# Moving query and key transposes to a projection bank, and leaving the projections two

## The chip, the cores and the metric

The kernel runs on one core of one Trainium2 chip. The metric is the device time of one execution in microseconds, from several runs; one further execution is profiled and gives the trace. In the profile the engines are PE (TensorE matmul, with PEld for its weight loads), DVE (VectorE), ACT (ScalarE), POOL (GpSimd) and SP (SyncE, which here issues most DMAs).

## The reference

One decoder layer over 512 tokens of width 1024, all in float32:

```
x = x + 0.5 * swiglu_ffn(x)                       # FFN 1
h = rms_norm(x)
fq, fk, fv, ff, dq, dk, dv, iq, ik, iw, ga, gb = split_columns(h @ w_in)
fq, fk = rms_norm(fq), rms_norm(fk)               # 8 heads of 64
o_a = fox_attention(fq, fk, fv, log_sigmoid(ff + b_forget))
o_b = dsa_attention(rms_norm(dq), rms_norm(dk), dv, iq, ik, iw, rel_bias)   # top-128 keys
x = x + (sigmoid(ga) * (o_a @ w_branch_a) + sigmoid(gb) * (o_b @ w_branch_b)) @ w_out
x = x + 0.5 * swiglu_ffn(x)                       # FFN 2
```

Each attention is causal: scores, a bias, softmax, and the weighted sum of values. `fox` has eight heads with their own keys and values, `dsa` eight heads that share one key and value head.

## The kernel before, in words

Every float32 operand is split in a high and a low part, and each product is three matmuls (`mm3`, lines 132 to 135: high by high, high by low, low by high). Tokens lie in four blocks of 128 (`NT`).

PSUM has eight banks of 128 x 512 floats. The kernel gives two to the tag `pt` (transposes), two to `s` (scores), one to `pv` (the sum of values, `po`) and three to `acc` (all products, through `acc_tile`). With three buffers under one tag, a new tile takes whichever buffer is free.

Between the two FFNs stands the mixing stage. The order of PE's instructions there is written out by hand; on the other engines a scheduler, which simulates the program when it is built, puts the instructions in order. The input projections and the later products are a list `units`, each a generator that yields after a few matmuls and says how long they take:

- unit 0: the small columns; 1 to 4: the indexer's queries (`fm_proj`, one bank each)
- 5 to 12: `fk0`, `fq0`, `fv0`, `fk1`, `fq1`, `fv1`, `dq0`, `dq1` (`tm_proj` through `tm256`, two banks each; the number is the half of the heads)
- then four gates, eight branch products, four more gates and four gates of the other branch (`fm_proj`, one bank each)

A `tm_proj` unit computes 512 tokens by 256 columns. Its first bank takes tokens 0 to 255, its second 256 to 511; it runs over two chunks of weights, in each over the four token blocks and four slices. So in the second chunk the first bank is complete eight product steps before the second. Then `done(ps)` reads the banks: `normed` scales them on ACT (L721), takes norms, and multiplies on POOL (L724); `values` reads each half bank once on ACT (L734) and once on DVE (L735).

`prod.run(us)` issues unit steps for about so many us between pieces of attention, `prod.finish(n)` runs units until n are done. The last steps before attention end unit 7 (`fv0`); a step that ends a unit may go on to the first product of the next one.

The attention loop goes over 16 heads `g` (8 fox, 8 dsa) and in each over four steps `s`, one query block each. A step does `value_step` (flip the probabilities of an earlier block by transposing into a `pt` bank, L925; copy them with ACT and DVE, L929 and L930; multiply by the values into `po`, L935 and L936), then `softmax_block` (scores into an `s` bank, L651 and L652; minimum on DVE, L914; exponential on ACT, L916; scaling on POOL, L918), then `prod.run(FILL[g])`. DVE also runs the selection of the top keys in between (L862, L864).

For every pair of heads, `get_q(g + 1)` transposes two heads' queries (`ps_q`, L626) into a `pt` bank, and reads them with ACT (L645) and DVE (L646) into `st`; `get_k(g + 1)` does so for the fox keys (`ps_k`, into `kh` and `kl`) and copies each half to the other partitions by DMA (L979, SP's queue). Before the change they follow steps 0 and 1 of every odd head. Weights are fetched three chunks ahead (`weight`, `load_w`: cast `wh` on ACT, L123; `wl`, on ACT at L125 with a DMA that adds, or on DVE or POOL at L128).

Of the kernel before, what the change touches and what calls it, by code (L numbers as in the profile page):

```python
# [18 lines left out]
P = 128  # L19
# [32 lines left out]
def tile_hybrid_layer(ctx: ExitStack, tc: tile.TileContext, a: dict):  # L52
# [10 lines left out]

    def acc_tile(name):
        return psum.tile([P, T], F32, tag="acc", bufs=3, name=name)

# [515 lines left out]
    with ExitStack() as merge_ctx, ExitStack() as mix_ctx, ExitStack() as att_ctx:  # L582
# [39 lines left out]

        def transposed(cols, name):
            ps = psum.tile([P, T], F32, tag="pt", bufs=2, name=name)
            for t in range(NT):
                PE.transpose(ps[:, t * P:(t + 1) * P], cols(t), ident)  # L626
            return ps
# [39 lines left out]

        def tm_proj(ws, cols, done):

            def run():  # L670
                ps = [acc_tile("ps_t")[:, :2 * cols].rearrange("p (u c) -> p u c", u=2) for _ in range(2)]
                for c in range(2):
                    wh, wl = ws[c]()
                    for t in range(NT):
                        for kk in range(4):
                            k = 4 * c + kk
                            mm3(ps[t // 2][:, t % 2], xh[k][:, t * P:(t + 1) * P], xl[k][:, t * P:(t + 1) * P],
                                wh[:, kk], wl[:, kk], k == 0 and t % 2 == 0, k == KD - 1 and t % 2 == 1)
                            if (c, t, kk) != (1, 3, 3):
                                yield MM / 2  # L680
                done(ps)
                yield MM / 2
            return run
# [14 lines left out]

        def small_done(ps):
            nonlocal rt  # L700
            rt = next(norm)
            for t in range(NT):
                p = ps[t // 2][:, t % 2]
                S.mul(sd[1][:, t], p[:, None, DH:2 * DH].to_broadcast([P, 2, DH]), rt[:, t:t + 1])
                S.mul(sg[:, t], p[:, 128:S_W], rt[:, t:t + 1])
                S.mul(sd[0][:, t], p[:, None, 0:DH].to_broadcast([P, 2, DH]), rt[:, t:t + 1])

                V.tensor_scalar(wi[:, t], sg[:, t, 72:80], rt[:, t:t + 1], DH ** -0.5 * H ** -0.5,
                                op0=OP.mult, op1=OP.mult)
# [4 lines left out]
        def normed(key):  # L714
            def done(ps):
                out = []
                for b in range(2):
                    kn = mp.tile([P, T], F32, tag="tn", bufs=8, name="kn")
                    kv = kn.rearrange("p (u c) -> p u c", u=2)
                    for u in range(2):  # L720
                        S.mul(kv[:, u], ps[b][:, u], rt[:, 2 * b + u:2 * b + u + 1])  # L721
                    r = qk_scale(kn, H)
                    kh = kn.rearrange("p (h d) -> p h d", d=DH)
                    G.tensor_mul(kh, kh, r[:, :, None].to_broadcast([P, H, DH]))  # L724
                    out.append(kv)
                tn[key] = out
            return done

        def values(hf):
            def done(ps):  # L730
                for t in range(NT):
                    vt = mp.tile([P, 4, P], F32R, tag=f"r{2 * t + hf}", name="fv")
                    src = ps[t // 2][:, t % 2].rearrange("p (h d) -> p h d", d=DH)
                    S.mul(vt[:, :, 0:DH], src, rt[:, t:t + 1])  # L734
# [19 lines left out]

        def tm256(name, n, done):
            return tm_proj([weight(a[name][n][:, 4 * c:4 * c + 4], 4, 256, W_AT, True) for c in range(2)], 256, done)

# [4 lines left out]
        units += [tm256("w_fk", 0, normed("fk0")), tm256("w_fq", 0, normed("fq0")), tm256("w_fv", 0, values(0)),  # L762
                  tm256("w_fk", 1, normed("fk1")), tm256("w_fq", 1, normed("fq1")), tm256("w_fv", 1, values(1)),
                  tm256("w_dq", 0, normed("dq0")), tm256("w_dq", 1, normed("dq1"))]
        n_fox = len(units)
# [185 lines left out]

        def columns(tiles, c, name):
            return transposed(lambda t: tiles[t // 2][:, t % 2, c * P:(c + 1) * P], name)

        def get_q(g):
# [3 lines left out]
            gain = gq[:, 0:1] if g < H else gq[:, 1:2]  # L959
            ps = columns(tn[f"{nm}{c // 2}"], c % 2, "ps_q")  # L960
            out = [at.tile([P, T], F32R, tag=tag, bufs=2, name="st") for tag in ("qh", "ql")]
# [5 lines left out]
        def get_k(g):  # L967
# [3 lines left out]
            c = g // 2  # L971
            ps = columns(tn[f"fk{c // 2}"], c % 2, "ps_k")
            out = []
# [71 lines left out]
        for g in range(2 * H):  # L1045
# [4 lines left out]
            for s in range(NT):  # L1050
# [10 lines left out]
                if g + 1 < 2 * H:  # L1061
                    if s == 0:
                        nb = get_bias(g + 1)
                    if s == 0 and g % 2:
                        nq = get_q(g + 1)
                    if s == 1 and g % 2:
                        nk = get_k(g + 1)
        for g, j in ((14, 3), (15, 0), (15, 1), (15, 2), (15, 3), (16, 0)):
            value_step(g, j)
            prod.run(FILL_LAST)  # L1070
        prod.finish(len(units))
        att_ctx.close()

# [118 lines left out]
```

## Time and profile before

| | us |
|---|---|
| median of 3 runs | 1090.99 (1089.07 to 1091.05) |
| the profiled execution | 1090.95 |
| its span, first to last instruction | 1088.9 |
| PE busy in the span | 1070.5 (98%) |
| DVE busy | 795.0 (73%) |
| ACT busy | 575.4 (53%) |
| POOL busy | 209.4 (19%) |
| mean granted TensorE clock | 0.998 |

A row of the trace names the line, the engine, the operation and, as out<-in, the tiles by the program's names; in brackets stands the idle time of the engine just before it and what ended that. `ps_t` and `ps_f` are the projection banks of `tm_proj` and `fm_proj`. A wait reads: who waited, at which line, for which engine's instruction.

### The profile page before, as it was taken

The page shows a single profiled execution, that of the slowest core. Times are in us where ns is not written, and L with a number is a line of the kernel's source. Part 1 is how long each engine was busy: PE and PEld are TensorE (multiplying, and loading weights), DVE is VectorE, ACT ScalarE, POOL GpSimd, SP SyncE. Part 2 cuts the span into 40 slices and gives each one's busy share as a digit, 9 for nine tenths or more (in the row PEclk, how much of TensorE's full clock was granted, in tenths as well). Part 3 has the DMA queues.
Part 4 walks back from the last instruction along what each step waited for, and adds up shares of the span by engine and source line. Part 5 has one row for each costly group of instructions (what it writes and reads, how often), then busy time and mean ns, then how long its engine had stood idle before and what let it go on. Part 6 is the DMA issues. An engine that isn't in the chain of part 4 may idle for free.

```text
span 1088.9 us, 17859 instructions
## 1 busy us (share of the span) xinstructions
PE 1070.5 (98%) x6880; PEld 968.1 (89%) x6880; DVE 795.0 (73%) x1287; ACT 575.4 (53%) x908; POOL 209.4 (19%) x280
## 2 busy tenths in 40 slices
PE   9999999999999999999999999999999999999998
PEld 7889899989998899988778778889998899989997
DVE  6896478755967489879764765879986588865974
ACT  5554155522555675877655785455663155522650
POOL 0000000000001316677752740000110001000100
PEclk9999999999999999999999999999999999999999
DMA  7434335523442268765124211425574356633552
GB/s 239 118 98 134 108 88 147 139 95 97 125 108 90 99 134 195 173 143 133 49 59 135 87 60 48 135 89 153 138 166 137 90 135 160 165 97 98 145 126 78
DMA packets 43572, 131.01 MB, mean 120 GB/s; under 512 B 5336, under 2 KB 5720, under 8 KB 43488
## 3 DMA queue, kind: packets, MB, share of 16 engines
q1 hardware_dynamic: 35120, 107.58, 32.5%
q0 software_dynamic: 8208, 22.02, 11.7%
q8 instruction: 54, 0.88, 0.3%
q10 hardware_dynamic: 160, 0.28, 0.1%
q14 instruction: 30, 0.25, 0.1%
HBM read 117.79 MB, written 2.11 MB: 110 GB/s over the span
## 4 chain that ended last, share of the span: by engine, by line
PE 85%; DVE 6%; ACT 4%; issue 2%; DMA 2%; POOL 1%; SPq 0%; DVEq 0%; POOLq 0%; ACTq 0%
PE pd L133 7%; PE pd L135 7%; PE pd L134 7%; PE pB L133 5%; PE pB L134 5%; PE pB L135 5%; PE pC L133 3%; PE pA L133 3%; PE pA L134 3%; PE pC L134 3%; PE pC L135 3%; PE pA L135 3%; PE ps_f L133 3%; PE ps_f L134 3%; PE ps_f L135 3%
## 5 line engine op out<-in xcount | busy, mean ns | idle before, releaser
L133 PE MATMUL pd<-ah,wh 128*128 128x512 f32 (+1 forms) x294 | 113.2, 385 | 0.0
L134 PE MATMUL pd<-al,wh 128*128 128x512 f32 (+1 forms) x294 | 113.1, 385 | 0.0
L135 PE MATMUL pd<-ah,wl 128*128 128x512 f32 (+1 forms) x294 | 113.1, 385 | 0.0
L112 ACT CAST wh<-s 128x1024 fp32r<-128x1024 f32 x57 | 60.1, 1054 | 99.1 <-PE pB L134 51.3
L133 PE MATMUL pB<-tbh,wh 128*128 128x256 f32 x304 | 85.0, 280 | 0.6 <-DVE u L435 0.6
L134 PE MATMUL pB<-tbl,wh 128*128 128x256 f32 x304 | 84.8, 279 | 0.0
L135 PE MATMUL pB<-tbh,wl 128*128 128x256 f32 x304 | 84.7, 279 | 0.0
L133 PE MATMUL ps_t<-wh,xh 128*128 128x256 f32 (+1 forms) x288 | 81.7, 284 | 0.0
L134 PE MATMUL ps_t<-wl,xh 128*128 128x256 f32 (+1 forms) x288 | 81.0, 281 | 0.0
L135 PE MATMUL ps_t<-wh,xl 128*128 128x256 f32 (+1 forms) x288 | 81.0, 281 | 0.0
L271 POOL DMA_DIRECT2D al<-gu x26 | 22.2, 856 | 260.5 <-ACT al L270 248.9
L113 DVE TENSOR_TENSOR wl<-s,wh 128x1024 fp32r<-128x1024 f32 x57 | 69.4, 1218 | 1.7 <-ACT wh L112 1.5
L393 POOL DMA_DIRECT2D s<-in_w_pair_dram x11 | 9.6, 877 | 297.9 <-DVE wl L113 297.9
L135 PEld LDWEIGHTS pd<-ah,wl 128*128 128x128 f32 x294 | 55.2, 188 | 11.1
L134 PEld LDWEIGHTS pd<-al,wh 128*128 128x128 f32 x294 | 55.2, 188 | 10.8
L133 PEld LDWEIGHTS pd<-ah,wh 128*128 128x128 f32 x294 | 55.2, 188 | 10.8
L133 PEld LDWEIGHTS pB<-tbh,wh 128*128 128x128 f32 x304 | 57.1, 188 | 1.1 <-issue 0.9
L134 PEld LDWEIGHTS pB<-tbl,wh 128*128 128x128 f32 x304 | 57.2, 188 | 0.0
L135 PEld LDWEIGHTS pB<-tbh,wl 128*128 128x128 f32 x304 | 57.2, 188 | 0.0
L134 PEld LDWEIGHTS ps_t<-wl,xh 128*128 128x128 f32 x288 | 55.1, 191 | 0.5
L133 PEld LDWEIGHTS ps_t<-wh,xh 128*128 128x128 f32 x288 | 55.0, 191 | 0.5
L135 PEld LDWEIGHTS ps_t<-wh,xl 128*128 128x128 f32 x288 | 55.0, 191 | 0.0
(355 smaller groups left out, 3611.9 us busy)
## 6 DMA issues: line engine op xcount, KB each, us to landing
rc<-in_w_pair_dram SPq DMA_DIRECT2D x16, 512.0 KB, 3.6
rb<-in_w_pair_dram SPq DMA_DIRECT2D x16, 512.0 KB, 3.6
ra<-in_w_pair_dram SPq DMA_DIRECT2D x15, 512.0 KB, 3.6
rd<-in_w_pair_dram SPq DMA_DIRECT2D x15, 512.0 KB, 3.7
re<-in_w_pair_dram SPq DMA_DIRECT2D x14, 512.0 KB, 3.7
al<-gu POOLq DMA_DIRECT2D x26, 256.0 KB, 4.7
s<-in_w_pair_dram POOLq DMA_DIRECT2D x11, 512.0 KB, 5.6
ra<-in_w_down_dram SPq DMA_DIRECT2D x7, 512.0 KB, 3.6
```

Of the source, the lines that this page charges most:

```text
L112: S.copy(wh[:, :f], raw[:, :f])
L113: V.tensor_sub(wl[:, :f], raw[:, :f], wh[:, :f].bitcast(F32))
L133: PE.matmul(out, lh, rh, start=start, stop=False, **more)
L134: PE.matmul(out, lh, rl, start=False, stop=False, **more)
L135: PE.matmul(out, ll, rh, start=False, stop=stop, **more)
L271: G.dma_start(l, u, accum_op=OP.add)
L393: G.dma_start(t["s2"], load["b"][2], accum_op=OP.add)
```

## The change

`acc_tile` no longer draws from a tag with three buffers: there are three tags `acc0`, `acc1`, `acc2` of one buffer each, taken in a fixed cycle or by name. The units `fk1`, `fq1`, `fv1`, `dq0` and `dq1` name acc0 and acc1, and set the cycle to these two, so that the gates and branch products after them use two banks as well; the cycle returns to three behind the attention loop. `get_q` and `get_k` for heads after the first transpose into acc2. Keys come first, after step 0 of an odd head, queries after step 2. `done(ps, b)` is called for each bank where its last product is issued. `get_k` makes sure that `fk1` is done before it reads it.

```diff
-    def acc_tile(name):
-        return psum.tile([P, T], F32, tag="acc", bufs=3, name=name)
+    acc_tags = {"next": cycle(("acc0", "acc1", "acc2"))}
+
+    def acc_tile(name, tag=None):
+        return psum.tile([P, T], F32, tag=tag or next(acc_tags["next"]), name=name)
...
-        def transposed(cols, name):
-            ps = psum.tile([P, T], F32, tag="pt", bufs=2, name=name)
+        def transposed(cols, name, tag=None):
+            ps = acc_tile(name, tag) if tag else psum.tile([P, T], F32, tag="pt", bufs=2, name=name)
...
-        def tm_proj(ws, cols, done):
+        def tm_proj(ws, cols, done, tags=(None, None)):
 
             def run():
-                ps = [acc_tile("ps_t")[:, :2 * cols].rearrange("p (u c) -> p u c", u=2) for _ in range(2)]
+                if tags[0]:
+                    acc_tags["next"] = cycle(tags)
+                ps = [acc_tile("ps_t", tag)[:, :2 * cols].rearrange("p (u c) -> p u c", u=2) for tag in tags]
...
-                            if (c, t, kk) != (1, 3, 3):
-                                yield MM / 2
-                done(ps)
-                yield MM / 2
+                            if (c, t % 2, kk) == (1, 1, 3):
+                                done(ps, t // 2)
+                            yield MM / 2
...
         units += [tm256("w_fk", 0, normed("fk0")), tm256("w_fq", 0, normed("fq0")), tm256("w_fv", 0, values(0)),
-                  tm256("w_fk", 1, normed("fk1")), tm256("w_fq", 1, normed("fq1")), tm256("w_fv", 1, values(1)),
-                  tm256("w_dq", 0, normed("dq0")), tm256("w_dq", 1, normed("dq1"))]
+                  *(tm256(name, n, done, ("acc0", "acc1"))
+                    for name, n, done in (("w_fk", 1, normed("fk1")), ("w_fq", 1, normed("fq1")), ("w_fv", 1, values(1)),
+                                          ("w_dq", 0, normed("dq0")), ("w_dq", 1, normed("dq1"))))]
...
-        def columns(tiles, c, name):
-            return transposed(lambda t: tiles[t // 2][:, t % 2, c * P:(c + 1) * P], name)
+        def columns(tiles, c, name, g):
+            return transposed(lambda t: tiles[t // 2][:, t % 2, c * P:(c + 1) * P], name, "acc2" if g else None)
...
-            ps = columns(tn[f"fk{c // 2}"], c % 2, "ps_k")
+            if c == 2:
+                prod.finish(9)
+            ps = columns(tn[f"fk{c // 2}"], c % 2, "ps_k", g)
...
                     if s == 0 and g % 2:
+                        nk = get_k(g + 1)
+                    if s == 2 and g % 2:
                         nq = get_q(g + 1)
-                    if s == 1 and g % 2:
-                        nk = get_k(g + 1)
...
         prod.finish(len(units))
+        acc_tags["next"] = cycle(("acc0", "acc1", "acc2"))
         att_ctx.close()
```

`small_done`, `normed` and `values` are split by bank in the same way: `values(hf)` reads the two token blocks of bank `b`, `normed(key)` appends one tile for each bank, and `small_done` does its work at the second.

More of the change, by code (lines that the diff above doesn't have):

```diff
@@ L697, in weight, with small_done @@
             return take
-        def small_done(ps):
+        def small_done(ps, b):
             nonlocal rt
+            if not b:
+                return
             rt = next(norm)
@@ L714, in normed, with done @@
         def normed(key):
[L715 to L726, printed above, removed]
+            def done(ps, b):
+                kn = mp.tile([P, T], F32, tag="tn", bufs=8, name="kn")
+                kv = kn.rearrange("p (u c) -> p u c", u=2)
+                for u in range(2):
+                    S.mul(kv[:, u], ps[b][:, u], rt[:, 2 * b + u:2 * b + u + 1])
+                r = qk_scale(kn, H)
+                kh = kn.rearrange("p (h d) -> p h d", d=DH)
+                G.tensor_mul(kh, kh, r[:, :, None].to_broadcast([P, H, DH]))
+                tn.setdefault(key, []).append(kv)
             return done
         def values(hf):
-            def done(ps):
-                for t in range(NT):
+            def done(ps, b):
+                for t in (2 * b, 2 * b + 1):
                     vt = mp.tile([P, 4, P], F32R, tag=f"r{2 * t + hf}", name="fv")
-                    src = ps[t // 2][:, t % 2].rearrange("p (h d) -> p h d", d=DH)
+                    src = ps[b][:, t % 2].rearrange("p (h d) -> p h d", d=DH)
                     S.mul(vt[:, :, 0:DH], src, rt[:, t:t + 1])
@@ L753, in keep_gate_b, with tm256 @@
             gb.append(g)
-        def tm256(name, n, done):
-            return tm_proj([weight(a[name][n][:, 4 * c:4 * c + 4], 4, 256, W_AT, True) for c in range(2)], 256, done)
+        def tm256(name, n, done, tags=(None, None)):
+            return tm_proj([weight(a[name][n][:, 4 * c:4 * c + 4], 4, 256, W_AT, True) for c in range(2)], 256, done,
+                           tags)
         oA = ([mp.tile([P, T], F32R, tag=f"oh{c}", name="oAh") for c in range(4)],
@@ L959, in get_q @@
             gain = gq[:, 0:1] if g < H else gq[:, 1:2]
-            ps = columns(tn[f"{nm}{c // 2}"], c % 2, "ps_q")
+            ps = columns(tn[f"{nm}{c // 2}"], c % 2, "ps_q", g)
             out = [at.tile([P, T], F32R, tag=tag, bufs=2, name="st") for tag in ("qh", "ql")]
```

## The prediction

> **What bounds the kernel now.** I read the page's busy shares first, then the waits of TensorE, then the timelines around the longest of them.
>
> ```profile
> PE 1070.5 (98%) x6880; PEld 968.1 (89%) x6880; DVE 795.0 (73%) x1287; ACT 575.4 (53%) x908; POOL 209.4 (19%) x280
> ```
>
> TensorE (PE) is busy for 1070.5 us of the span. Everything that this change can win lies in the other 18 us, and every new wait of PE adds to the end, because PE runs its instructions in the order written. The waits say who ends that idle time (columns: waiter, its line, whom it waited for; total us, times, longest):
>
> ```profile
> core 0 of [0], span 1088.9 us
> PE pt L925 <- DVE st L646: 2.7, 3, 1.7
> PE ps_qk L651 <- DVE mn L914: 2.2, 2, 1.2
> PE pt L925 <- DVE pl L930: 1.8, 3, 0.9
> PE po L936 <- DVE pl L930: 1.3, 3, 0.9
> PE po L935 <- DVE o L948: 1.1, 3, 0.6
> ...
> PE ps_k L626 <- DVE pl L930: 0.8, 1, 0.8
> ```
>
> All of these lie in the attention loop. The first row is the one that the change is about: a probability flip (`pt`) needs one of the two `pt` banks, and a bank still holds a transposed query until DVE has read it (`st`, L646). The third and the last row are the same conflict from other sides: a flip or the key transpose (`ps_k`) waits until DVE has emptied the other flip's bank (`pl`). One place of each kind, the second with what follows it:
>
> ```profile
> 452.80 0.66 PE L626 MATMUL ps_k<-ident,kn 128*128 128x128 f32 x4 [0.81 <-DVE pl L930]
> 454.18 0.55 PE L925 MATMUL pt<-ident,p 128*128 128x128 f32 x3 [0.72 <-DVE st L646]
> ...
> 561.31 0.55 PE L925 MATMUL pt<-ident,p 128*128 128x128 f32 x3 [0.93 <-DVE pl L930]
> 562.51 0.50 PE L935 MATMUL po<-ph,dvv 128*128 128x512 f32 x1 [0.65 <-DVE o L948]
> ```
>
> **Part 1: later queries and keys leave the `pt` banks.** Seven query and three key transposes go to bank acc2. The three rows `pt <- st`, `pt <- pl` and `ps_k <- pl` lose their cause: 2.7 + 1.8 + 0.8 = 5.3 us. That is the upper end; not all of it stays won. Behind 454.18 PE needs `pl` of the flip before it, behind 561.31 it waits for DVE again (0.65 us at `o`), and the row `po <- pl` (1.3 us) is DVE arriving late at the place where PE will now be earlier. I give back 1.3 us, the size of that row: net -4.0. Lower end: half is given back, -2.7; upper end: -5.3. The waits for `mn` (2.2) I leave where they are, since they are DVE's own lateness.
>
> **Part 2: keys in step 0, queries in step 2.** The same transposes, ACT copies and DVE subtractions run, only at another step; ACT takes 0.68 us and DVE 0.75 us for each half (rows below). Each key brings four copies on SP's queue, each query none:
>
> ```profile
> kh<-kh SPq DMA_DIRECT2D x8, 128.0 KB, 2.7
> kl<-kl SPq DMA_DIRECT2D x8, 128.0 KB, 3.4
> ```
>
> They move one step earlier, ahead of that step's weight loads in SP's queue, and land 3.4 us after issue, now with three steps before the key is used instead of two. Cost nothing. The query keeps one step where it had three. A step is worth
>
> ```profile
> L651 PE MATMUL ps_qk<-kh,st x32: 220/312/497, 434.5 to 540.2; 128*128 128x512 f32 x8, 128*128 128x384 f32 x8, 128*128 128x256 f32 x8, 128*128 128x128 f32 x8
> ```
>
> (540.2 - 434.5) / 31 = 3.4 us. The next head needs only the first half of the query: 0.66 for four transposes, 0.68 ACT, 0.75 DVE, so 2.1 us if nothing stands in front. The cover of 3.4 us holds it with 1.3 us left; if the cover goes, `ps_qk` waits. I count it at 0 inside the 1.3 us above, between 0 and some 2 us over all seven.
>
> **Part 3: each projection bank emptied once complete.** This moves the place in the program where the reading of the first bank is written down, not the work. Before the change, ACT already reads the first bank of a unit when it is complete: in the last unit before attention (`fv0`) at 431.08, while PE ends that unit near 434.3.
>
> ```profile
> 434.01 0.28 PE L135 MATMUL ps_t<-wh,xl 128*128 128x256 f32 x1
> 434.12 0.28 PE L133 MATMUL ps_t<-wh,xh 128*128 128x256 f32 x1
> ```
>
> ```profile
> 431.08 0.47 ACT L734 ACTIVATE fv<-ps_t,rstd 128x256 fp32r<-128x256 f32 x1 [0.66 <-PE ps_t L135]
> ...
> 434.32 1.05 ACT L123 CAST wh<-rc 128x1024 fp32r<-128x1024 f32 x1 [1.74 <-PE ps_t L135]
> 435.28 0.47 ACT L734 ACTIVATE fv<-ps_t,rstd 128x256 fp32r<-128x256 f32 x1
> 435.77 0.68 ACT L645 ACTIVATE st<-ps_q,gq 64x512 fp32r<-64x512 f32 x1
> 436.48 1.06 ACT L125 ACTIVATE wl<-wh 128x1024 fp32r<-128x1024 f32 x1
> ...
> 438.85 0.72 ACT L916 ACTIVATE p<-p,mn 128x512 f32<-128x512 f32 x1
> ...
> 439.69 0.47 ACT L734 ACTIVATE fv<-ps_t,rstd 128x256 fp32r<-128x256 f32 x1
> ```
>
> ```profile
> 435.87 0.48 DVE L735 SCALAR_TENSOR_TENSOR fv<-ps_t,rstd,fv 128x256 fp32r<-128x256 f32 x1
> 436.49 0.75 DVE L646 SCALAR_TENSOR_TENSOR st<-ps_q,gq,st 64x512 fp32r<-64x512 f32 x1
> ...
> 440.91 0.47 DVE L735 SCALAR_TENSOR_TENSOR fv<-ps_t,rstd,fv 128x256 fp32r<-128x256 f32 x1
> ```
>
> So Part 3 gains nothing by itself; it only makes two banks nearly as good as three.
>
> **Part 4: two banks instead of three.** Here the new wait is. Banks now follow a fixed cycle, so one can count. FFN 1 draws 10 tiles for its plain columns, 3 for each pair and 8 for each of three groups of down products:
>
> ```profile
> L133 PE MATMUL pA<-b1h,wh x64: 277/279/283, 75.3 to 302.0; 128*128 128x256 f32 x64
> ```
>
> 64 such products at 8 in a pair are 8 pairs, so 10 + 24 + 24 = 58 tiles. The first projection unit takes 58 and 59, the four indexer units 60 to 63, `fk0` 64 and 65, `fq0` 66 and 67, `fv0` 68 and 69. Tile 69 is acc0 (69 divides by 3). The next unit, `fk1`, must start in acc0: the bank that `fv0` has just finished. With three banks it started in the free one, and PE went on at 434.12 without a gap. Now its first product waits until acc0 is read by four instructions in turn (ACT, DVE, ACT, DVE; in the timelines each ACT reading of a bank comes after the DVE reading before it). In PE's order the first scores of attention stand behind this product, so they wait too, and with them their softmax.
>
> How long? In the profile that chain ends with DVE at 440.91 + 0.47 = 441.38, 7.3 us after 434.12: the upper end. But the exponential at 438.85 cannot stand in between now, since its scores are not there. Then ACT's order is weight cast to 435.37, first reading to 435.75, query to 436.45, `wl` to 437.54, second reading to 438.01, DVE 0.48 more, and a hop of 0.05 on either side: PE goes on at 438.6, 4.5 us late. If the scheduler puts the readings ahead of everything else, 0.47 + 0.48 + 0.47 + 0.48 and four hops are 2.1 us after 434.29, 2.3 us late: the lower end. I take 4.5, since the order of the weight cast and of `wl` is decided by things that do not change.
>
> A long stall has a second price. The granted clock fell once in this stage (columns: stretch, length, busy and count of PE, weight loads, DVE, ACT, POOL; clock, DMA):
>
> ```profile
> 418.51:421.92 3.41, 3.41 (x33) 3.41 (x32) 3.38 (x12) 3.41 (x7) 2.42 (x3) 1.00 0.84 239
> 421.92:425.34 3.42, 3.42 (x18) 3.42 (x18) 3.34 (x8) 0.71 (x2) 1.24 (x2) 0.50 0.88 141
> ```
>
> For 3.4 us the clock was 0.50, with 18 products instead of 33, so 3.4 x (1 - 18/33) = 1.5 us lost, after a stretch in which PE had never been idle but ran transposes and tiny products. If even light work does that, a stretch that is mostly idle does it the more: I add 1.5 us (0 to 1.7, half of 3.4).
>
> [...]
>
> The other changes of unit also go from three banks to two, but there eight product steps and attention work lie between the last write of a bank and its next. One place is short:
>
> ```profile
> 489.59 0.28 PE L133 MATMUL ps_t<-wh,xh 128*128 128x256 f32 x1
> ```
>
> ```profile
> 490.61 0.48 ACT L734 ACTIVATE fv<-ps_t,rstd 128x256 fp32r<-128x256 f32 x1
> ```
>
> ```profile
> 491.13 0.48 DVE L735 SCALAR_TENSOR_TENSOR fv<-ps_t,rstd,fv 128x256 fp32r<-128x256 f32 x1
> ```
>
> `dq0` first writes its second bank at 489.59, while `fv1` has that bank read at 491.61: 2.0 us late in the worst case, 0 if the readings move up with PE waiting; I take 0.8. The gates and branch products after it take one bank each, and a whole unit lies between two uses of a bank; I count them at nothing, and if ACT or DVE come later than one unit, that cover is gone.
>
> **Sum**, against the profiled execution's own 1090.95 us (2.05 over its span; the median of the runs is 1090.99): -5.3 + 1.3 + 4.5 + 1.5 + 0.8 = +2.8, so 1093.75, say 1093.7.
>
> **The rivals.** Short stall: the scheduler orders ACT and DVE anew, and puts both readings of acc0 ahead of the weight cast. Then 2.3 us and no clock loss: -5.3 + 1.3 + 2.3 + 0.8 = -0.9, 1090.05, not slower. It decides where PE goes on before 437.5. For it: ACT was idle for 1.74 us just before the cast, so the order there is not tight; against it: the cast is written with raised priority.
>
> Short stall and no give-back: as before, and DVE keeps up, with the query's work out of step 0: -5.3 + 2.3 = -3.0, 1087.95, faster. For it: at 562.51 the wait for `o` stands right behind a query copy, which moves away. Against it: the `po <- pl` waits.
>
> [...]
>
> Long stall: the readings keep their place of 441.38: 7.3 for 4.5, 1096.55. For it, the profile's own order; against it, the exponential's absence.
>
> The change may also do less than it says: its third part does nothing by itself, as shown.
>
> **Chances.** Forecast 0.33 (own range 1092.5 to 1095.5), long stall 0.12, stall without clock loss 0.17, short stall 0.16, short stall without give-back 0.22. About 0.2% (2.2 us) is what a measurement of this kernel can tell from no change: slower 0.45, same 0.33, faster 0.22. The range runs from 1087.7 (just under the fastest case) to 1097.0 (the long stall and a little of the late bank).
>
> **What would show it.** Right: no wait `pt <- st` and no `ps_k` wait in the profile after; a new wait of PE before the first `ps_t` product of the attention loop, released by DVE `fv` L735, of 3 to 5 us; a stretch of clock 0.50 near 440; a smaller wait of the same kind near 490. Wrong: the stall under 2 us or not there (the banks then fall otherwise than I counted), new waits of `ps_qk` for `st` at the heads' starts, or a gap of several us in `ps_f` from the gates' two banks.

## The result, and the profile after

The changed kernel takes 1102.03 us (median, 1101.16 to 1105.68); the kernel before took 1090.24 us beside it. The ratio is 1.0109 [1.0092, 1.0125]: slower by 11.8 us of the medians, where +2.8 was forecast. The profiled execution of it took 1102.01 us, its span is 1100.3, which is 11.4 us more than before.

First PE's busy time in the page after:

```profile
PE 1074.0 (98%) x6880; PEld 971.3 (88%) x6880; DVE 799.5 (73%) x1287; ACT 574.9 (52%) x908; POOL 213.0 (19%) x280
```

The same instructions, and 3.5 us more of busy PE (1070.5 before), at a mean granted clock of 0.995 (0.998 before): products at a lower clock count as longer work (one of 256 columns took 0.42 us in the median between 439.8 and 444.8, at a clock of 0.50, and 0.28 between 400 and 433, at 1.00). The rest of the 11.4 us of span is idle time, and PE's waits after say where:

```profile
PE ps_t L135 <- DVE fv L737: 6.6, 2, 5.5
PE po L940 <- DVE pl L934: 4.5, 8, 1.3
PE ps_qk L653 <- DVE mn L918: 3.0, 2, 2.2
PE pt L929 <- POOL p L922: 2.6, 3, 1.8
...
PE po L939 <- DVE o L952: 1.4, 2, 0.9
```

(Lines are two to four higher than before.) The rows `pt <- st`, `pt <- pl` and `ps_k <- pl`, 5.3 us together, are gone as forecast. New is `ps_t <- fv`, the wait for a bank, 5.5 us at `fk1` and 1.1 at `dq0`. And the rows for `pl`, `mn`, `p` and `o`, which summed to 1.3 + 2.2 + 0.6 + 1.1 = 5.2 before, now sum to 11.5: 6.3 us more.

The stall at `fk1`, on PE, ACT and DVE of the changed kernel:

```profile
433.39 0.28 PE L137 MATMUL ps_t<-wh,xl 128*128 128x256 f32 x1
439.18 0.55 PE L135 MATMUL ps_t<-wh,xh 128*128 128x256 f32 x1 [5.52 <-DVE fv L737]
```

```profile
433.70 1.04 ACT L125 CAST wh<-rc 128x1024 fp32r<-128x1024 f32 x1
434.65 0.47 ACT L736 ACTIVATE fv<-ps_t,rstd 128x256 fp32r<-128x256 f32 x1
435.15 0.68 ACT L647 ACTIVATE st<-ps_q,gq 64x512 fp32r<-64x512 f32 x1
435.85 1.06 ACT L127 ACTIVATE wl<-wh 128x1024 fp32r<-128x1024 f32 x1
436.93 0.47 ACT L736 ACTIVATE fv<-ps_t,rstd 128x256 fp32r<-128x256 f32 x1
```

```profile
434.53 1.11 DVE L737 SCALAR_TENSOR_TENSOR fv<-ps_t,rstd,fv 128x256 fp32r<-128x256 f32 x2
435.86 0.76 DVE L648 SCALAR_TENSOR_TENSOR st<-ps_q,gq,st 64x512 fp32r<-64x512 f32 x1 [0.22 <-ACT st L647]
...
437.05 1.47 DVE L866 MAX8 m<-sc 128x8 f32<-128x384 f32 x3
438.55 0.48 DVE L737 SCALAR_TENSOR_TENSOR fv<-ps_t,rstd,fv 128x256 fp32r<-128x256 f32 x1
```

ACT's order is the forecast one: cast, reading, query, `wl`, reading. The last reading ends on ACT at 437.40, but DVE is then in three instructions of the selection and reads the bank only at 438.55. Then the clock (columns as in the prediction):

```profile
435.00:438.40 3.40, 0.00 (x0) 0.00 (x0) 3.01 (x8) 3.31 (x5) 1.64 (x4) 0.94 0.94 300
438.40:441.80 3.40, 2.62 (x10) 2.45 (x11) 3.28 (x11) 0.31 (x1) 0.42 (x2) 0.50 0.86 152
441.80:445.20 3.40, 3.40 (x19) 3.40 (x18) 0.24 (x3) 0.81 (x2) 0.69 (x1) 0.55 0.33 99
445.20:448.60 3.40, 3.40 (x30) 3.40 (x29) 1.91 (x7) 0.71 (x2) 0.58 (x1) 1.00 0.00 0
...
540.80:544.20 3.40, 3.40 (x13) 2.82 (x12) 1.20 (x3) 1.95 (x4) 3.40 (x6) 0.55 0.00 0
```

Half the clock for some 6.8 us after the stall, and once more for about 3.4 us near 541.

**Where the 11.4 us arise.** The table gives how much later than before (us, negative is earlier) a unit's first product starts in each profiled execution, from the rows of `ps_t` and `ps_f` in order; "gate 4" is the last of the four gates that follow `dq1`, and "growth" is gate 4 less `dq1`, a stretch of 47 us before. "Idle" is how much longer PE stands idle within this stretch than before, "at 0.50" how long the granted clock is halved in it. The kernels of the other rows are those of the experiments below.

| kernel | fv0 | fk1 | fq1 | dq0 | dq1 | gate 4 | growth | idle | at 0.50 | end |
|---|---|---|---|---|---|---|---|---|---|---|
| changed | 0.58 | 5.06 | 7.68 | 5.15 | 6.00 | 11.04 | 5.0 | 2.5 | 3.4 | 11.36 |
| turned cycle | 0.06 | 0.07 | 0.08 | -2.35 | -0.88 | 5.72 | 6.6 | 4.0 | 3.4 | 6.35 |
| spare products | -0.34 | 4.17 | 4.26 | 1.80 | 2.65 | 7.70 | 5.1 | 1.8 | 3.4 | 8.29 |
| places alone | 0.40 | -1.14 | -0.73 | -2.50 | -2.00 | 0.65 | 2.7 | 1.3 | 3.4 | 1.77 |
| cycle and readings by bank alone | 0.30 | 0.32 | 0.32 | -0.79 | -0.25 | 1.20 | 1.5 | 1.1 | 0 | 2.25 |
| two readings in a row | -0.19 | 2.87 | 5.64 | 2.15 | 3.01 | 5.89 | 2.9 | 0.1 | 3.4 | 6.97 |
| turned, old places | 0.57 | -0.62 | 0.19 | 2.06 | 5.18 | 5.85 | 0.7 | 0.3 | 0 | 5.64 |
| turned, readings at the end | 0.20 | -1.34 | -0.91 | -3.21 | -1.85 | 2.21 | 4.1 | 2.4 | 3.4 | 2.39 |
| turned, gates off DVE | 0.34 | -0.82 | -0.06 | -2.48 | -1.03 | -0.16 | 0.9 | 0.2 | 0 | -0.01 |
| changed, gates off DVE | -0.11 | 4.37 | 6.91 | 4.44 | 5.27 | 6.18 | 0.9 | 0.2 | 0 | 6.27 |
| before, gates off DVE | 0.98 | 1.00 | 1.00 | 1.21 | 1.21 | 0.36 | -0.9 | -1.4 | 0 | 2.76 |
| turned, gates on POOL | 0.83 | 0.87 | 0.87 | -1.61 | -0.19 | 9.80 | 10.0 | 6.0 | 10.2 | 10.40 |
| gates off DVE, one operand | -0.02 | -1.22 | -0.40 | -2.89 | -1.44 | 3.22 | 4.7 | 2.1 | 3.4 | 4.43 |
| gates off DVE, two operands | 0.61 | -0.59 | 0.22 | -2.26 | -0.80 | 4.84 | 5.6 | 2.8 | 3.4 | 4.94 |
| turned, end, gates off DVE | 0.97 | -0.57 | -0.16 | -2.32 | -1.02 | -1.06 | 0.0 | -0.6 | 0 | -0.56 |

The first row read from left to right is the sum of the change: 0.58 was there before attention; the stall is 5.52, of which 1.04 comes back because the clock does not drop near 421 as it did before (5.06 - 0.58 = 4.48); the halved clock costs 7.68 - 5.06 = 2.62; the removed waits give 2.53 back up to `dq0`; the late bank there costs 0.85; and then 5.04 are lost up to gate 4, and 0.32 after it. So there are two losses of like size, the stall with its clock and the stretch of the gates. Where a profiled execution has no drop of the clock near 421, as this one, it gains 1.0 to 1.5 us by `fk1` through the clock (the places alone: from 0.40 to -1.14); the turned cycle has the drop, as the kernel before has.

**The second loss is waits and clock together.** The stretch of the gates, from `dq1` to gate 4, before, changed, and in the turned cycle, its version with the gates off DVE, that with one further operand of DVE, and the one with the gates on POOL (columns as in the prediction):

```profile
503.79:550.93 47.14, 43.20 (x274) 38.13 (x273) 35.90 (x88) 33.14 (x77) 38.14 (x55) 1.00 0.24 67
509.79:561.97 52.18, 45.75 (x274) 39.44 (x273) 38.13 (x91) 33.26 (x77) 40.78 (x55) 0.97 0.21 66
502.90:556.65 53.75, 45.80 (x275) 39.61 (x274) 39.16 (x91) 33.31 (x77) 40.75 (x55) 0.97 0.21 63
502.76:550.77 48.01, 43.90 (x275) 38.04 (x273) 31.74 (x87) 37.58 (x83) 41.35 (x59) 1.00 0.50 111
502.35:554.15 51.80, 45.79 (x274) 39.65 (x273) 35.73 (x91) 37.37 (x83) 41.23 (x59) 0.97 0.46 103
503.60:560.73 57.13, 47.17 (x274) 41.38 (x273) 34.24 (x87) 33.29 (x79) 46.68 (x59) 0.91 0.20 56
```

PE makes the same products in each, so the length is its busy time and its idle time. In the changed kernel both grow, by 2.55 us busy and 2.49 idle. Where the clock stays whole, PE's busy time is 0.4 to 0.7 us above before; where it is halved for 3.4 us, 1.4 to 3.3 us. So a drop is some 1 to 2 us of a growth (an estimate from these rows), and the waits are the rest. DVE is busy for 69 to 76% of the stretch in the first three and the fifth: 35.90 us of its work go with a length of 47.14 before, and 35.73 us with 51.80 in the fifth row, so the sum of DVE's work doesn't say how long the stretch takes.

### The profile page after: what moved, and what is told of

Same layout as the page of the kernel before. It is cut to its first block, busy times and chain, and to the rows that moved or that the text cites. A ratio compares the mean times of both kernels' runs of the same rounds, so it can differ in the third digit from the quotient of the medians.

```text
span 1100.3 us, 17857 instructions
## 1 busy us (share of the span) xinstructions
PE 1074.0 (98%) x6880; PEld 971.3 (88%) x6880; DVE 799.5 (73%) x1287; ACT 574.9 (52%) x908; POOL 213.0 (19%) x280
## 4 chain that ended last, share of the span: by engine, by line
PE 85%; DVE 5%; ACT 3%; POOL 3%; issue 2%; DMA 1%; SPq 0%; DVEq 0%; POOLq 0%; ACTq 0%
PE pd L135 7%; PE pd L137 7%; PE pd L136 7%; PE pB L135 5%; PE pB L136 5%; PE pB L137 5%; PE pC L135 3%; PE pC L137 3%; PE pC L136 3%; PE pA L135 3%; PE pA L137 3%; PE pA L136 3%; PE ps_f L135 3%; PE ps_f L136 3%; PE ps_f L137 2%
```

## The experiments

Each group of experiments was timed on a chip of its own, with the kernel before beside it, so two experiments are compared by their ratios to that; one thousandth is 1.1 us.

**The turned cycle** (the bank theory). The first tile of the program draws acc2 instead of acc0, so that `fv0` ends in acc1 and acc2 and `fk1` starts in the free acc0; nothing else changes.

```diff
-    acc_tags = {"next": cycle(("acc0", "acc1", "acc2"))}
+    acc_tags = {"next": cycle(("acc2", "acc0", "acc1"))}
```

> The changed kernel with the cycle of banks started at acc2, so that fv0 takes acc1 and acc2, and fk1's first bank, acc0, is the free one; nothing else differs. Theory A (the bank that fv0 has just finished costs a stall of 5.5 us and a halved clock for 6.8 us, some 2.6 us; the rest of the loss comes from the moved keys and queries): no wait of ps_t for fv at fk1, no clock of 0.50 near 440, 1102.0 - 8.1 = about 1094, still 3 to 4 us slower than before. Theory B (the later waits po<-pl, pt<-p and ps_qk<-mn are only what the stall set off): they go too, 1088 to 1090.

1096.64 us (1095.31 to 1097.94), ratio 1.0047 [1.0033, 1.006]. The wait at `fk1` and the halved clock behind it are gone: 0.07 in the table. By `dq0` PE is 2.35 us ahead of before: the removed waits do give something. That is 5.4 us of the 11.8 by the medians (6.8 by the ratios), so the bank that the prediction counted is the cause of that part. But from `dq1` to gate 4 the kernel falls back by 6.6 us, and it ends 6.35 late. Theory A is right about the bank and 2.6 us too low about the time; theory B falls. PE's waits between 500 and 560 us:

```profile
PE po L940 <- DVE pl L934: 3.7, 3, 2.0
PE ps_qk L653 <- DVE mn L918: 2.2, 1, 2.2
PE pt L929 <- POOL p L922: 1.8, 1, 1.8
```

One of them in detail, on DVE, POOL and PE:

```profile
535.92 4.17 DVE L130 TENSOR_TENSOR wl<-rb,wh 128x1024 fp32r<-128x1024 f32 x1 [0.16 <-ACT wh L125]
540.02 1.15 DVE L934 TENSOR_TENSOR pl<-pt,ph 128x512 fp32r<-128x512 f32 x2
```

```profile
535.64 0.69 POOL L922 TENSOR_SCALAR p<-p,rs 128x512 f32<-128x512 f32 x1
536.33 1.40 POOL L998 TENSOR_SCALAR b<-cb,ncum 128x384 f32<-128x384 f32 x3
537.71 1.26 POOL L1002 TENSOR_TENSOR b<-sc,cb 128x512 f32<-128x512 f32 x1
538.93 1.31 POOL L999 TENSOR_SCALAR_AFFINE_SELECT b<-b 128x128 f32<-128x128 f32 x1
```

```profile
540.75 0.50 PE L940 MATMUL po<-pl,fv 128*128 128x512 f32 x1 [2.04 <-DVE pl L934]
```

The subtraction of a gate's weights takes 4.17 us on DVE while POOL runs without a pause; `pl`, for which PE waits 2.04 us, stands behind it. The kernel before had the same subtraction at the same place in 1.48:

```profile
L128 DVE TENSOR_TENSOR wl<-rb,wh x1: 1481/1481/1481, 534.2 to 534.2; 128x1024 fp32r<-128x1024 f32 x1
```

**Spare products in the stall** (the clock's price). Twenty products that nothing uses, into the bank of `po`, ahead of `fk1`'s first product.

```diff
+                        warm = psum.tile([P, T], F32, tag="pv", name="warm")
+                        for _ in range(20):
+                            PE.matmul(warm, xh[0][:, 0:P], xh[0], start=True, stop=True)
```

> The changed kernel with 20 spare products of 512 columns (some 4.6 us) written into the still unused bank of po ahead of fk1's first product, so that PE computes instead of standing still; the result doesn't use them. If the halved clock is set off by the idle stretch, the clock stays at 1.00 near 440 and the time falls by 2.5 to 3 us, to about 1099.3; if the stall alone is the price, it stays at 1102 within 1 us.

```profile
432.60 4.72 PE L680 MATMUL warm<-xh 128*128 128x512 f32 x20
```

```profile
436.90:440.30 3.40, 2.42 (x17) 1.95 (x16) 3.37 (x11) 0.92 (x1) 1.04 (x3) 1.00 1.01 261
```

No drop of the clock there, and from `fk1` to `fq1` 0.09 us are lost instead of 2.62, so that is what the halved clock costs. The median does not follow: 1102.19 (1098.15 to 1103.82), ratio 1.0096 [1.0077, 1.0115]. The profiled execution is one of two at a mean clock of 0.998 (1098.15, 1098.93); the others, at 0.996 and 0.995, took 1101.92 or more, so they lost clock at some other place, which no trace of them shows.

**Two readings in a row** (how long the stall must be). In the changed kernel ACT reads both halves of a bank and then DVE both, instead of ACT, DVE, ACT, DVE.

```diff
-                for t in (2 * b, 2 * b + 1):
-                    S.mul(vt[:, :, 0:DH], src, rt[:, t:t + 1])
-                    mark(V.scalar_tensor_tensor(...), 1.5)
+                for t in both:
+                    S.mul(fv[t, hf][:, :, 0:DH], src[t % 2], rt[:, t:t + 1])
+                for t in both:
+                    mark(V.scalar_tensor_tensor(...), 1.5)
```

> The changed kernel; only the reading of a finished bank of values is written in another order: both ACT readings first, then both DVE readings, so that the bank changes hands once instead of three times. fk1 still starts in the bank that fv0 has just finished. Theory A (the stall is the length of the hand-over ACT, DVE, ACT, DVE with what lies in between in both queues): the stall of 5.5 us falls to 2 to 3.5 us, the clock stays at 1.00 near 440 or falls more rarely, and the time is 1096 to 1098. Theory B (the readings simply come late, behind weight casts and selection): stall 4.5 us or more, 1101 to 1103.

```profile
436.99 0.55 PE L135 MATMUL ps_t<-wh,xh 128*128 128x256 f32 x1 [2.88 <-DVE fv L740]
```

```profile
434.11:436.14 2.03, 0.01 (x1) 0.00 (x0) 0.18 (x2) 1.96 (x4) 1.07 (x4) 1.00 1.00 220
436.14:442.96 6.82, 5.97 (x26) 5.80 (x27) 6.14 (x18) 3.66 (x5) 2.09 (x4) 0.50 0.87 195
```

1097.36 us (1093.63 to 1101.71), ratio 1.0061 [1.004, 1.0083]. The stall falls to 2.88 us and the wait at `dq0` vanishes; the clock is halved all the same, after 2.03 us of the stall, and costs 2.8 us (`fk1` to `fq1`). So theory A's shorter stall came, but not the whole clock that it hoped for. A stall of 2.3 us, the prediction's short one, was not run.

**Two parts alone, on the kernel before.** First only the places: keys after step 0, queries after step 2, both still in the `pt` banks, with three free `acc` banks (and the check that `fk1` is done before its keys are read).

```diff
                     if s == 0 and g % 2:
-                        nq = get_q(g + 1)
-                    if s == 1 and g % 2:
                         nk = get_k(g + 1)
+                    if s == 2 and g % 2:
+                        nq = get_q(g + 1)
```

> The kernel before with one part of the change alone: keys follow step 0 and queries step 2 of odd heads, still in the pt banks, three projection banks, banks read as before. Theory A: the moved steps bring new waits of po for pl and of pt for p, beyond the waits for st that stay: 1093 to 1095. Theory B: the place of the steps costs nothing by itself: 1090 within 1.5 us.

1092.31 (1090.4 to 1094.72), ratio 1.001 [0.9999, 1.0021]: between the two forecasts, and no difference that can be told. Its profiled execution is 2.5 us ahead at `dq0`, 1.5 of it for want of the drop near 421, and loses that again in the stretch of the gates, where the clock is halved once. Then only the cycle of three named banks and the reading of each bank where it is complete:

```diff
-                            if (c, t, kk) != (1, 3, 3):
-                                yield MM / 2
-                done(ps)
-                yield MM / 2
+                            if (c, t % 2, kk) == (1, 1, 3):
+                                done(ps, t // 2)
+                            yield MM / 2
```

> The changed kernel with everything undone but two parts: banks by a fixed cycle of three, and the reading of each bank written where its last product is issued. Queries and keys are transposed into pt after steps 0 and 1, as before. The engines read a complete bank at once in the kernel before as well, so both theories expect 1090 within 2 us; if the place in the program does change ACT's and DVE's order for the worse, 1092 to 1095.

1093.89 (1092.27 to 1098.37), ratio 1.0027 [1.0016, 1.0039]. The part that was to cost nothing costs some 2.9 us, the named cycle and the early readings together. One piece of it has a name: the cycle starts anew behind attention and comes upon a bank that was just used.

```profile
661.45 0.50 PE L135 MATMUL ps_gb<-xh,wh 128*128 128x512 f32 x1 [0.61 <-DVE gb L754]
```

**The same parts undone, on the turned cycle.** Old places, still in acc2:

```diff
                     if s == 0 and g % 2:
-                        nk = get_k(g + 1)
-                    if s == 2 and g % 2:
                         nq = get_q(g + 1)
+                    if s == 1 and g % 2:
+                        nk = get_k(g + 1)
```

> The cycle started at acc2, queries and keys in acc2, but at their old places: queries after step 0, keys after step 1 of odd heads. If the moved steps bring the later waits (po for pl, pt for p, ps_qk for mn), these go and the time is 1091 to 1093. If they come whatever the step, because POOL and DVE set the pace around 500 to 545 us, it stays at 1096.6 within 1.5 us.

1094.75 (1094.02 to 1097.34), ratio 1.0041 [1.0026, 1.0056], between the two forecasts. Keys wait for the query's reading of their common bank (`ps_k <- st`, 4.7 us), and `dq0` waits 2.5 us for the bank of `fv1`, so PE is 5.18 us late at `dq1`; the gates then add only 0.7. Readings written at the unit's end again:

```diff
-                            if (c, t % 2, kk) == (1, 1, 3):
-                                done(ps, t // 2)
-                            yield MM / 2
+                            if (c, t, kk) != (1, 3, 3):
+                                yield MM / 2
+                for b in range(2):
+                    done(ps, b)
+                yield MM / 2
```

> The cycle started at acc2, and the reading of both banks of a unit written at the unit's end as in the kernel before; keys, queries and the two banks as in the changed kernel. If writing the readings at each bank's end costs something by its place in the program (the run with that part and the cycle alone was 2.9 us slower than before), 1093.5 to 1095; if not, 1096.6 within 1 us.

```profile
515.89 0.33 PE L653 MATMUL ps_qk<-kh,st 128*128 128x128 f32 x1 [3.93 <-DVE mn L920]
```

1094.09 (1093.18 to 1097.08), ratio 1.0036 [1.0022, 1.0049]: 2.5 us less than the turned cycle by the medians, but only 1.2 by the ratios, whose intervals overlap. The wait of 3.93 us had not been there. The order of ACT, DVE and POOL is made anew by the scheduler with every edit, so each of them moves waits about; 2 us of one edit alone can't be put down to a cause.

**Without the bank wait at `dq0`.** The turned cycle with two readings in a row, and the same with readings at the end:

> Both edits: the cycle started at acc2 (fk1 finds a free bank) and both ACT readings ahead of both DVE readings. The wait of 1.7 us for fv1's bank at dq0, which the run with the cycle alone still had, should fall under 0.8 us; 1096.6 - 1 = about 1095.6. If the time stays at 1096.6 within 0.5 us although that wait is gone, PE only meets a later wait sooner.

> The cycle started at acc2, the readings written at the unit's end (the run of 1094.1), and both ACT readings of values ahead of both DVE readings. The wait of 1.6 us at dq0 should go: 1094.1 - 1.0 = about 1093. If the time stays at 1094 within 0.5 us though the wait is gone, the next late engine takes it back.

1095.93 (1093.41 to 1096.86), ratio 1.0041 [1.0025, 1.0056], and 1095.94 (1095.11 to 1097.01), ratio 1.0054 [1.004, 1.0067]. Both lose the wait at `dq0` and neither is faster for it beyond what can be told: their growth is 5.5 and 4.0 us. The first came out near its forecast, the second 3 us above. The bank wait at `dq0` is not what bounds.

**The gates' weights off DVE.** The low parts of the four early gates' weights are made by ACT and a DMA that adds, on POOL's queue, instead of DVE. On the turned cycle, on the kernel before, and on the changed kernel:

```diff
-        gates = [fm_proj(weight(a["w_ga"][d], KD, P), (xh, xl), KD, keep_gate) for d in range(EARLY_GATES)]
+        gates = [fm_proj(weight(a["w_ga"][d], KD, P, 0, True), (xh, xl), KD, keep_gate) for d in range(EARLY_GATES)]
```

> The cycle started at acc2 (the run of 1096.6), and one more edit: the low parts of the four early gates' weights are made by ACT and an adding DMA from POOL's queue instead of by DVE, as for the keys' and queries' weights. In the run of the cycle alone one such DVE subtraction took 4.17 us at 536 while POOL ran without a pause, and the next wait of PE for DVE (po for pl, 2.0 us) stood behind it. If DVE, slowed by POOL there, sets the pace at 530 to 545 us, that wait falls under 0.5 us and the time to 1093.5 to 1095; if PE is held by POOL's biases and probabilities as such, 1096 to 1097, with the wait elsewhere.

> The kernel before with the gates' weights made by ACT and the adding DMA: the control for that edit. There the same subtractions took 1.2 to 1.5 us; 1090.5 within 1.5 us, at best 1089.

> The changed kernel with one edit: the low parts of the four early gates' weights made by ACT and the adding DMA instead of by DVE; fk1 still starts in the bank just finished. If the loss has two separate parts (the stall with its clock, 5.4 us by the run of the cycle alone; DVE at the gates, 5.7 us by the run with both edits), this gives 1102.0 - 5.7 = 1096.3 within 1 us. If the second part only shows once the first is gone, 1099 to 1102.

On the turned cycle 1090.90 (1090.3 to 1092.28), ratio 1.0008 [1.0, 1.0017]: 5.7 us less by the medians, 4.3 by the ratios, and better than either forecast. Its waits of PE between 500 and 560 us:

```profile
PE pt L929 <- POOL p L922: 2.4, 3, 1.0
PE po L940 <- DVE pl L934: 1.0, 2, 0.7
PE ps_qk L653 <- DVE mn L918: 0.7, 2, 0.4
```

They fall from 7.7 to 4.1 us, the clock stays whole, and the growth is 0.9 instead of 6.6. On the changed kernel 1098.13 (1097.35 to 1099.22), ratio 1.0071 [1.0058, 1.0084], growth 0.9 instead of 5.0; the stall at `fk1` stays. That is 4.1 us less by the ratios, as on the turned cycle, though 1.8 us above the forecast. On the kernel before the same edit costs: 1092.18 (1090.73 to 1094.19), ratio 1.002 [1.001, 1.003]. So the second loss belongs to the change and to DVE's work in this stretch together, and the two losses can be taken away one by one: the gates' edit is worth 4.1 and 4.3 us with the stall and without it, the turned cycle 6.8 and 6.9 us without the gates' edit and with it.

**The same work on POOL.** On the turned cycle, the four subtractions on POOL:

```diff
+            if by_dma == "pool":
+                G.tensor_sub(wl[:, :f], raw[:, :f], wh[:, :f].bitcast(F32))
```

> The cycle started at acc2, and the same four subtractions made by POOL instead of DVE, with no DMA and nothing more for ACT. If DVE's own load sets the pace around 520 to 545 us, 1091.5 to 1094; if POOL's does, the subtraction (a 128x1024 one, some 2 to 2.5 us each on POOL) makes it worse: 1097 or more.

```profile
529.54 5.04 DVE L956 TENSOR_TENSOR oAl<-o,oAh 64x512 fp32r<-64x512 f32 x1 [0.34 <-ACT oAh L955]
```

```profile
529.13 2.39 POOL L127 TENSOR_TENSOR wl<-ra,wh 128x1024 fp32r<-128x1024 f32 x1
531.52 1.50 POOL L1000 TENSOR_SCALAR b<-cb,ncum 128x256 f32<-128x256 f32 x3
532.99 1.04 POOL L729 TENSOR_TENSOR kn<-kn,rh 128x512 f32<-128x512 f32 x1
534.02 1.00 POOL L924 TENSOR_SCALAR p<-p,rs 128x384 f32<-128x384 f32 x1
```

```profile
535.55 0.38 PE L942 MATMUL po<-pl,fv 128*128 128x256 f32 x1 [3.85 <-DVE pl L936]
```

1101.01 (1099.45 to 1103.01), ratio 1.0099 [1.0083, 1.0114]: growth 10.0, with the clock halved for 10.2 us of the stretch. DVE has less to do and is later still: a subtraction whose eight executions take 0.75 us in the median in the changed kernel takes 5.04 us beside a run of POOL work that the moved one lengthens.

**Time or place?** Two kernels on the turned cycle with the gates off DVE ask what DVE lacked. The first gives DVE a further instruction per weight of the same length with one operand from SBUF, the second one with two; nothing uses the results.

```diff
+                    V.tensor_reduce(raw[:, :8], wh[:, :f].bitcast(F32).rearrange("p (h d) -> p h d", h=8), axis=AX.X, op=OP.add)
```

```diff
+                    V.tensor_sub(raw[:, :f], raw[:, :f], wh[:, :f].bitcast(F32))
```

> The kernel with the turned cycle and the four gates' low parts by ACT and an adding DMA (1090.90 us), to which DVE gets one further instruction for each of the four weights: a sum over the 1024 columns of the high part into 8 columns of the raw buffer, which nothing uses. It takes DVE about as long as the subtraction that was taken away (1.2 us, estimated from 0.67 us for 512 columns), with a single operand from SBUF. Theory A (what DVE lost was not time but its place: an instruction with both operands in SBUF stands until a run of POOL instructions ends, as the 4.17 us of a subtraction and the 5.04 us of another one show, while those with one operand in PSUM kept to 0.70 us): the time stays, 1090.0 to 1092.5, and no row of the sum is above 1.5 us. Rival B (DVE was short of time, 4 x 1.2 us): most of the 5.7 us comes back, 1095 to 1097.

> As the one before, but the further instruction of DVE is a subtraction of 128x1024 with both operands in SBUF (raw less high part, into the raw buffer, which nothing uses). PE waits for none of its results. Theory A: some of the four are stretched to 2 to 5 us while POOL runs without a pause, the waits of PE for pl, p and mn grow with that, and the time goes to 1094 to 1097. Rival B: the same as with one operand, whatever that gives, within 1 us. If it stays near 1091 with no row above 1.5 us, the subtractions fell beside a pause of POOL, and nothing is told apart.

Two of the four added instructions of the one and of the other (ns: shortest, median, longest; the other two took 1219 and 1220, and 1267 and 1348):

```profile
L128 DVE TENSOR_REDUCE rb<-wh x2: 1219/1220/1220, 502.8 to 536.5; 128x8 f32<-128x1024 f32 x2
```

```profile
L128 DVE TENSOR_TENSOR rb<-rb,wh x2: 1224/1885/2546, 503.5 to 538.2; 128x1024 f32<-128x1024 f32 x2
```

One operand: 1095.08 (1093.55 to 1095.68), ratio 1.0039 [1.0025, 1.0053]. Two: 1098.73 (1095.59 to 1099.64), ratio 1.0074 [1.0059, 1.0088]. Theory A alone falls: 4 x 1.22 us of DVE, never stretched, cost 4.2 us by the medians and 3.4 by the ratios. In the stretch of the gates that is 1.9 us more of idle PE and 1.9 us more of busy PE, the second with a drop of the clock that the kernel without the added work did not have (0.97 against 1.00 in the rows above). So DVE's time counts here, although DVE is not full.

With two operands it is 3.7 us more, the intervals apart, which is also above theory A's own 1094 to 1097. One added row takes 2.55 us beside POOL (the shortest 1.22). But how the 3.7 us are made up is not shown: the profiled execution was the quickest of the six, and at its clock of 0.998 the two kernels are only 0.5 to 0.7 us apart (1095.59 against 1094.85 and 1095.08); its other five, at 0.993 to 0.996, took 1096.91 or more, and no trace shows where their clock fell.

**Towards a version that wins.** Three more: turned cycle, readings at the end, two in a row, gates off DVE; the same with the other eight gates off DVE as well; and the first without the two readings in a row.

> All four edits together: cycle started at acc2, readings written at the unit's end, ACT readings first, gates' weights off DVE. If each edit frees what it says, 1090 to 1092, level with the kernel before; if the stretch from 500 to 545 us is paced by DVE and POOL whatever the banks, 1093 or more.

> The run with all four edits (1090.8), and the weights of the other eight gates also made by ACT and the adding DMA. In that run two of these subtractions still took 1.1 us longer on DVE than the others, near 597 and 646, with waits of PE for DVE of 0.4 to 0.9 us around them. If those waits go, 1089 to 1090; if ACT's and the DMA's extra work takes it back, 1091.

> The turned cycle, readings written at the unit's end, and the four gates' low parts by ACT and an adding DMA; the values are read as in the changed kernel. Alone on the turned cycle the readings at the end gave 2.5 us and the gates 5.7 us. If the two add, 1088.4, 2 us under the kernel before. If both cure the same waits, 1090 to 1091, as with the third edit beside them (1090.79).

1090.79 (1088.84 to 1092.76), ratio 1.0004 [0.9994, 1.0013]; 1098.31 (1096.26 to 1099.76), ratio 1.0072 [1.0058, 1.0087]; 1090.11 (1088.55 to 1091.63), ratio 0.9994 [0.9985, 1.0004]. The last has no growth at all and ends 0.56 us ahead in the profile, where its clock stays whole and that of the kernel before fell near 421: level with the kernel before, not faster beyond what can be measured. By the ratios the readings at the end gave 1.2 and 1.5 us, without the gates' edit and with it; the intervals overlap both times. The second shows the other end: it has no growth up to gate 4 either (nor has the first), but then the low part of a later gate, now made by ACT and POOL's queue of DMAs, comes late.

```profile
591.71 0.79 PE L137 MATMUL ps_f<-xh,wl 128*128 128x512 f32 x1 [5.48 <-DMA wl<-in_w_ga_dram]
```

## Why the prediction was right in its sign and wrong in its size

- **The count of banks was right.** `fk1` had to start in the bank that `fv0` had just finished; turning the cycle by one took the stall away (0.07 at `fk1`) and nothing else was needed.
- **The stall, term 4.5.** Measured 5.52 of idle time, above the 3 to 5 us that were named as its sign; 4.48 net of the drop near 421 that the kernel before had and this one has not. That 4.48 lies so near 4.5 is luck. ACT's order was as written out; left out were the three instructions of the selection on DVE ahead of the last reading.
- **The clock, term 1.5.** Measured 2.6: two lengths of 3.4 us, where one was counted. The clock fell at 438.01, when PE had stood idle from 433.67 on. A stall without a loss of clock, which had a chance of 0.17, did not come: in each of the three kernels with a wait at `fk1` and no products put in it (changed, two readings in a row, changed with the gates off DVE) 2.5 to 2.8 us go from `fk1` to `fq1`, in the second although its whole stall is 2.88 us.
- **Part 1, "I give back 1.3 us". This step failed.** The 5.3 us went as forecast, and 2.5 of them show as a lead gained up to `dq0`. But 6.3 us came back in `po <- pl`, `mn`, `p` and `o`, and a stretch of half the clock near 541 with them, a price that the prediction put at nothing outside the stall: from -4.0 the term went to -2.53 + 5.04 + 0.32 = +2.8, which is 6.8 us of the 8.6 us missed (11.4 less 2.8). The clock behind the stall is 1.1 us of the rest, the late start 0.6. The row `po <- pl` of 1.3 us was taken for the measure of DVE's lateness, on the ground that DVE is late where PE comes earlier. That ground fails too: the changed kernel comes to `dq1` 6.0 us later than before and still loses 5.04 us behind it. What the runs showed in its place: between `dq1` and gate 4 PE waits longer for DVE and POOL when DVE also makes the gates' low parts. In all five kernels of the change in which ACT and a DMA make these, with no other work put on DVE, the growth is 0.9 us or less and the clock stays whole there; 4 x 1.22 us of other work put on DVE bring 3.8 us of growth back.
- **Part 3, "gains nothing by itself".** It gains nothing, but with the named cycle it costs: +2.9 us, of which the late `ps_gb` explains 0.6. The prediction looked at the one unit where ACT's order stayed. In the run with these parts alone PE waits for `mn` 3.3 us instead of 2.2, and `pt` for `pl` 3.0 instead of 1.8; that the early readings push these back is likely and not shown.
- **`dq0`, term 0.8.** Measured 0.85 (a wait of 1.09 us). Taken away, it gives nothing that can be told; the stretch behind it is long all the same.
- **Part 2, term 0.** Right within what can be told (1.001 [0.9999, 1.0021]); no wait of `ps_qk` for `st` appears in the changed kernel.
- **0.58 us** of the profiled execution's lateness lie ahead of attention, where the change does nothing.

It stays open why the gates' work on DVE costs 0.9 us of that stretch in the kernel before and 4.1 in the changed one; in the sum DVE has nearly the same work there (35.90 and 38.13 us). The places alone grow by 2.7 us in that stretch and the cycle and readings by bank alone by 1.5, the two together with two banks and acc2, on a cycle without a stall, by 6.6. That is what the runs show; a cause in the scheduler's order was not isolated.

## What to carry to other kernels

A removed wait is worth no more than the engines behind it let through in the same stretch. Neither the size of their present waits (1.3 us here, 6.3 came back) nor the sum of their work (35.90 us of DVE in 47.14, 35.73 in 51.80) was the bound, so try it: take work off the engine, and put as much idle work back. Count a wait's price in clock as well (2.6 us behind the 5.52 us here). When banks go from "whichever is free" to a fixed cycle, count the tiles to the place of the change, since one step of the cycle decided 6.8 us here by the ratios. Work moved off a vector engine must be moved to where there is time; the same four subtractions were worth -4.3 us on ACT and DMAs and +5.7 on POOL, by the ratios.

## What the runs showed of the hardware

**Some DVE instructions took several times longer beside POOL work.** A subtraction of 1024 columns with both operands in SBUF, which takes 1.22 us in the median, took 4.17 us beside unbroken POOL work, and 2.55 when added for the purpose; one of 512 columns (0.75 in the median of the changed kernel) took 5.04. Those with an operand in PSUM did not, as all 64 of `pl` in the turned cycle show:

```profile
L934 DVE TENSOR_TENSOR pl<-pt,ph x64: 271/484/693, 452.1 to 665.0; 128x512 fp32r<-128x512 f32 x16, 128x384 fp32r<-128x384 f32 x16, 128x256 fp32r<-128x256 f32 x16, 128x128 fp32r<-128x128 f32 x16
```

In the changed kernel 11 of the 16 `pl` of 512 columns ran with POOL busy for over 95% of their time, and took at most 0.69 us. The 5.04 us outlast five POOL instructions in a row (2.39 + 1.50 + 1.04 us). That a subtraction stands until a run of POOL work ends, as theory A of the last question (time or place) has it, the rows do not show: the one of 4.17 us ended at 540.09, and POOL went on without a pause to 542.22. Nor is every one longer: at 521.80 in the changed kernel a subtraction of 1024 columns with both operands in SBUF took 1.22 us with POOL busy throughout. And two operands are not the only case: a TENSOR_SCALAR on `ss` (128x8, one operand in SBUF) takes 0.14 to 0.17 us with POOL idle and took 0.90 at 412.02 in the changed kernel, POOL being busy for 0.86 of it. What decides between them no run here shows.

**The clock was halved behind shorter waits than the stall, too.** With the two readings in a row it fell to 0.50 when PE had been idle for 2.03 us; with spare products in the stall it stayed at 1.00. In the changed kernel it was at 0.50 from 438.01 to 444.84, behind 3.41 us without any work of PE, and from 540.41 to 543.83, where PE had been idle for 2.15 of the 3.41 us before. With one operand it fell near 516.4, and PE was idle for 1.86 us of the stretch from 513.60 to 517.00. It stayed at 1.00 in the changed kernel with 1.83 us of idle PE from 512.00 to 515.41, and in the kernel before with 1.67 from 509.45 to 512.86. And near 422 it fell in the kernel before without any idle time in the 3.41 us ahead, behind products of 8 columns. So in this kernel waits that come to some 2 us close together cost clock as well; how much idle time that takes is not shown.
